# The normalisation of x in whole [128, 1024] tiles, its squares on ScalarE and its sums on VectorE

## The chip, the cores and the metric

The kernel runs on one core of a Trainium2 chip. Its time is the device time of one execution in microseconds; a figure for a kernel is the median of several executions. Engines are called as in the profile: PE is TensorE (matrix products), PEld its loading of weights, DVE is VectorE, ACT is ScalarE, POOL is GpSimd, SP is SyncE, which here issues the transfers.

## The reference, cut to what matters

One layer of an encoder works on `x` of 1024 tokens by 2048 features in float32. The input is normalised by its root mean square and multiplied by one large matrix, whose columns are split into the attention's parts and those of a state space model:

```
def rms_norm(x, g):
    y = x * rsqrt(mean(x * x, axis=-1) + EPS)
    return y * g

hn = rms_norm(h, norm_mix[i])
z = hn @ w_in[i]                      # 2048 x 4608
q, k, v, gate_a, u, gate_s = split(z)
```

Attention, the state space model, two more projections and a final norm follow; the change doesn't touch them.

## The kernel before, in words

The features lie on the partitions: `x` is 16 tiles of 128 features by 1024 tokens (step k = 0 to 15), and a column of the projection is 128 outputs. The kernel multiplies in two parts to keep float32 accuracy: a matrix X is split into H (X rounded to the type in which PE multiplies) and L (what is left of it), and a product is the sum of H·H, H·L and L·H. So a step k of a column is six products of 128 x 512, three for each half of the tokens (`mm_k`, lines 513 to 522): the weight's `wH` with `hH` (line 519) and `hL` (line 520), its `wL` with `hH` (line 522).

The scale by the gain `g` is folded into the split of `x`: `split` (lines 303 to 311) has ScalarE make `hH` = g·x (line 310) and VectorE make `hL` = g·x - `hH` (line 311). Weights go through the same helper without a gain: `wH` by ScalarE (line 307), `wL` by VectorE (line 308). The division by the root mean square comes later, on the columns' results. For it the squares of `x` are summed over the 16 tiles into `xsq` (128 x 1024) by `x_sq`; a product with ones then adds over the partitions (`x_rstd`, `colsum`).

The stage in question is the first loop of `run`. Two columns, `zf0` and `zf1`, are worked on at the same time, so a step is twelve products. Weights come in tiles of four steps each, two tiles (one for each column) for a block of four steps. In step k the program issues, in this order, the two columns' products, the load of tile k + 4 (`x_dma`), the split of tile k + 2 (`x_split`) and the square of tile k + 1 (`x_sq`); at k = 0, 4, 8, 12 `w_next` first loads and splits weights. Every engine takes its instructions in the order of the program, and waits where an operand or a buffer is not ready.

Three rings of buffers couple the engines. `xraw` has ten half tiles of 128 x 512, so a load of x waits until the tile five steps before has been split and squared. `wraw` has three tiles, so a weight load waits for the `wL` of an earlier tile; SyncE issues loads of x and of weights from one queue, and a waiting weight load holds up the loads of x behind it. `wH` and `wL` have four tiles each, so the casts for the next block wait until PE has finished the block before the current one's.

Before the change everything about x is done in half tiles: two loads, two `hH`, two `hL`. The first half of the tokens is squared and added by GpSimd (lines 493 and 495), the second half is squared by ScalarE (line 491) and added by VectorE (line 495). In step 0 ScalarE writes the squares of both halves straight into `xsq` (line 487).

Behind the stage come the third column (`zt`), with the parameters of the state space model as background work, the other columns, attention and the later projections.

Of the kernel before, what the change touches and what calls it, by code (L numbers as in the profile page):

```python
# [9 lines left out]
F32 = mybir.dt.float32  # L10
F32R = mybir.dt.float32r
I32 = mybir.dt.int32
ALU = mybir.AluOpType
AF = mybir.ActivationFunctionType
AX = mybir.AxisListType

SEQ = 1024
# [221 lines left out]
class Kernel:  # L239
# [223 lines left out]
    def x_dma(self, k):  # L463
        if k >= KD:
            return
        for h in range(2):
            xt = self.xp.tile([128, 512], F32, name="xraw", tag="xraw", bufs=10)
            self.nc.sync.dma_start(xt, self.i["xT"][k][:, self.half(h)])
            self.xraw.append(xt)

    def x_split(self, k):
        H = self.b4(f"hH{k}", dt=F32R)
        L = self.b4(f"hL{k}", dt=F32R)
        self.hH.append(H)
        self.hL.append(L)
        for h in range(2):
            s = self.half(h)
            self.split(H[:, s], L[:, s], self.xraw[2 * k + h], self.g_mix[:, k : k + 1])

    def x_sq(self, k):  # L480
        nc = self.nc
        for h in range(2):
            s = self.half(h)
            xt = self.xraw[2 * k + h]
            self.xraw[2 * k + h] = None
            if k == 0:
                nc.scalar.activation(self.xsq[:, s], xt, AF.Square)
                continue
            sq = self.xp.tile([128, 512], F32, name="xq", tag="xq", bufs=4)
            if h:  # L490
                nc.scalar.activation(sq, xt, AF.Square)
            else:
                nc.gpsimd.tensor_tensor(sq, xt, xt, ALU.mult)
            eng = nc.vector if h else nc.gpsimd
            eng.tensor_tensor(self.xsq[:, s], self.xsq[:, s], sq, ALU.add)

    def x_rstd(self):
        self.rstd = self.xsq
# [907 lines left out]
```

## Time and profile before

| | |
|---|---|
| median of 3 runs | 2195.66 us (2195.22 to 2196.39) |
| the profiled execution | 2196.16 us |
| its span | 2194.4 us |
| PE busy in it | 2129.4 us |
| DVE, ACT, POOL busy | 1384.1, 780.0, 656.0 us |

The span runs from the first to the last instruction that the profiler saw; the execution's time is 1.8 us longer. The products of PE overlap, so the distance between two starts says more than the duration of one. A row of the timeline merges neighbouring instructions of a kind (x2); the bracket at its end is the idle time of the engine before it and what ended it.

### The profile page before, as it was taken

How to read it: one execution, taken by the hardware profiler on the slowest of the kernel's cores; microseconds unless marked ns; L12 is line 12 of the kernel's file. 1: busy time of each engine (PE TensorE's matmuls, PEld its weight loads, DVE VectorE, ACT ScalarE, POOL GpSimd, SP SyncE). 2: the span in 40 equal slices, each digit the busy share in tenths (PEclk: the TensorE clock that was granted, in tenths of full speed). 3: DMA queues.
4: the chain of work that ended last, by engine and by line, in shares of the span. 5: the costliest groups of instructions: out<-in, count | busy, mean ns of one | idle time of the engine just before them, and what ended most of it. 6: DMA issues, size and time to landing. Idle time of an engine off the chain costs nothing.

```text
span 2194.4 us, 29198 instructions
## 1 busy us (share of the span) xinstructions
PE 2129.4 (97%) x10428; PEld 1777.3 (81%) x10428; DVE 1384.1 (63%) x2292; ACT 780.0 (36%) x1438; POOL 656.0 (30%) x630
## 2 busy tenths in 40 slices
PE   7999999999999999999999999999999999999996
PEld 5788878888887888887889888888887788888885
DVE  8745678787878787847999744444444644444344
ACT  5211222222222222237777633333334333333332
POOL 6152455555655554601222100111122000111120
PEclk8999999999999999999999999999999999999998
DMA  5224223323323333342121244444343644453333
GB/s 193 85 99 124 65 76 90 94 87 85 105 81 97 87 93 86 97 150 75 39 77 39 92 137 137 146 151 124 124 139 119 213 142 144 144 153 114 126 113 125
DMA packets 173313, 245.08 MB, mean 112 GB/s; under 512 B 27376, under 2 KB 77680, under 8 KB 172912
## 3 DMA queue, kind: packets, MB, share of 16 engines
q1 hardware_dynamic: 173168, 243.22, 35.6%
q8 instruction: 82, 1.34, 0.2%
q14 instruction: 63, 0.52, 0.1%
HBM read 189.35 MB, written 48.56 MB: 108 GB/s over the span
## 4 chain that ended last, share of the span: by engine, by line
PE 49%; DVE 3%; ACT 1%; DMA 1%; issue 1%; POOL 0%; DVEq 0%; SPq 0%; ACTq 0%
PE ph L1046 5%; PE ph L1047 5%; PE ph L1045 5%; PE pg L1047 5%; PE pg L1046 5%; PE pg L1045 5%; PE ptr L955 2%; PE pv L969 1%; PE pv L968 1%; PE pv L970 1%; PE S L925 1%; PE S L928 1%; PE S L924 1%; PE gg L1047 1%; PE gv L1047 1%; PE gv L1046 1%
## 5 line engine op out<-in xcount | busy, mean ns | idle before, releaser
L308 DVE TENSOR_TENSOR wL<-wraw,wH 128x512 fp32r<-128x512 f32 (+1 forms) x496 | 408.5, 844 | 451.1 <-ACT wH L307 449.5
L307 ACT CAST wH<-wraw 128x512 fp32r<-128x512 f32 (+1 forms) x496 | 294.0, 604 | 461.1 <-PE ph L1046 124.1
L1045 PE MATMUL pg<-hg,wH 128*128 128x512 f32 x512 | 200.8, 392 | 1.6 <-ACT wH L307 1.6
L1047 PE MATMUL pg<-hg,wL 128*128 128x512 f32 x512 | 199.9, 390 | 0.7 <-DVE wL L308 0.7
L1046 PE MATMUL pg<-hg,wH 128*128 128x512 f32 x512 | 199.7, 390 | 0.0
L1113 POOL TENSOR_TENSOR xsq<-xsq,tz 128x512 f32<-128x512 f32 x30 | 39.0, 1301 | 517.8 <-ACT tz L1112 517.8
L837 ACT COPY ks<-kp 16x224 f32<-16x224 f32 x32 | 10.8, 336 | 340.3 <-DVE ks L836 189.2
L1045 PEld LDWEIGHTS pg<-hg,wH 128*128 128x128 f32 x512 | 96.3, 188 | 22.4 <-ACT wH L307 2.0
L1047 PEld LDWEIGHTS pg<-hg,wL 128*128 128x128 f32 x512 | 96.4, 188 | 21.1 <-DVE wL L308 1.2
L1046 PEld LDWEIGHTS pg<-hg,wH 128*128 128x128 f32 x512 | 96.4, 188 | 20.5 <-issue 0.5
L519 PE MATMUL zga<-hH,wH 128*128 128x512 f32 x256 | 104.0, 406 | 0.0
L519 PE MATMUL zq<-hH,wH 128*128 128x512 f32 x256 | 103.5, 404 | 0.0
L519 PE MATMUL zgs<-hH,wH 128*128 128x512 f32 x256 | 102.6, 401 | 0.0
L520 PE MATMUL zq<-hL,wH 128*128 128x512 f32 x256 | 100.7, 394 | 0.0
L520 PE MATMUL zgs<-hL,wH 128*128 128x512 f32 x256 | 100.4, 392 | 0.0
L520 PE MATMUL zga<-hL,wH 128*128 128x512 f32 x256 | 100.2, 391 | 0.0
L1045 PE MATMUL ph<-ma,wH 128*128 128x512 f32 x256 | 99.6, 389 | 0.0
L1046 PE MATMUL ph<-ma,wH 128*128 128x512 f32 x256 | 99.6, 389 | 0.0
L1047 PE MATMUL ph<-ma,wL 128*128 128x512 f32 x256 | 99.6, 389 | 0.0
L1045 PE MATMUL ph<-ms,wH 128*128 128x512 f32 x256 | 99.6, 389 | 0.0
L1046 PE MATMUL ph<-ms,wH 128*128 128x512 f32 x256 | 99.6, 389 | 0.0
L1047 PE MATMUL ph<-ms,wL 128*128 128x512 f32 x256 | 99.6, 389 | 0.0
(420 smaller groups left out, 5432.6 us busy)
## 6 DMA issues: line engine op xcount, KB each, us to landing
wraw<-in_w_in_dram SPq DMA_DIRECT2D x144, 256.0 KB
wraw<-in_w_out_dram SPq DMA_DIRECT2D x128, 256.0 KB
wraw<-in_w_gate_dram SPq DMA_DIRECT2D x128, 256.0 KB
wraw<-in_w_glu_dram SPq DMA_DIRECT2D x64, 256.0 KB
xraw<-in_xT_dram SPq DMA_DIRECT2D x32, 256.0 KB
out_dram<-h SPq DMA_DIRECT2D x32, 256.0 KB
t<-zz SPq DMA_DIRECT2D x40, 128.0 KB
d_u<-tz SPq DMA_DIRECT2D x16, 256.0 KB
```

The lines of the kernel that those rows point to most:

```text
L307: nc.scalar.copy(H, src)
L308: nc.vector.tensor_tensor(L, src, H.bitcast(F32), ALU.subtract)
L519: nc.tensor.matmul(ps[h], H[:, kk, :], rH[:, s], start=(k == 0), stop=False)
L520: nc.tensor.matmul(ps[h], H[:, kk, :], rL[:, s], start=False, stop=False)
L924: nc.tensor.matmul(S[:, s], qH[:, qs], kH[:, s], start=True, stop=False)
L925: nc.tensor.matmul(S[:, s], qH[:, qs], kL[:, s], start=False, stop=False)
L928: nc.tensor.matmul(S[:, s], qL[:, qs], kH[:, s], start=False, stop=True)
L955: nc.tensor.transpose(pc[:, b], P[:, 512 * hf + 128 * b : 512 * hf + 128 * b + 128], self.ident)
L1045: nc.tensor.matmul(ps, H[:, k % 4], x[:, 0], start=(k == 0), stop=False)
L1046: nc.tensor.matmul(ps, H[:, k % 4], x[:, 1], start=False, stop=False)
L1047: nc.tensor.matmul(ps, L[:, k % 4], x[:, 0], start=False, stop=(k == nk - 1))
L1113: nc.gpsimd.tensor_tensor(acc, acc, s2, ALU.add)
```

## The change

A tile of x is one buffer of 128 x 1024 (five of them), filled by one load, split by one instruction on each engine and squared by one on ScalarE; VectorE adds the whole square into `xsq`. Only tile 0 is still loaded and split in two halves. GpSimd has no part in it any more.

```diff
     def x_dma(self, k):
         if k >= KD:
             return
-        for h in range(2):
-            xt = self.xp.tile([128, 512], F32, name="xraw", tag="xraw", bufs=10)
-            self.nc.sync.dma_start(xt, self.i["xT"][k][:, self.half(h)])
-            self.xraw.append(xt)
+        xt = self.xp.tile([128, SEQ], F32, name="xraw", tag="xraw", bufs=5)
+        for s in [self.half(0), self.half(1)] if k == 0 else [slice(0, SEQ)]:
+            self.nc.sync.dma_start(xt[:, s], self.i["xT"][k][:, s])
+        self.xraw.append(xt)
 
     def x_split(self, k):
...
-        for h in range(2):
-            s = self.half(h)
-            self.split(H[:, s], L[:, s], self.xraw[2 * k + h], self.g_mix[:, k : k + 1])
+        for s in [self.half(0), self.half(1)] if k == 0 else [slice(0, SEQ)]:
+            self.split(H[:, s], L[:, s], self.xraw[k][:, s], self.g_mix[:, k : k + 1])
 
     def x_sq(self, k):
         nc = self.nc
-        for h in range(2):
-            s = self.half(h)
-            xt = self.xraw[2 * k + h]
-            self.xraw[2 * k + h] = None
-            if k == 0:
-                nc.scalar.activation(self.xsq[:, s], xt, AF.Square)
-                continue
-            sq = self.xp.tile([128, 512], F32, name="xq", tag="xq", bufs=4)
-            if h:
-                nc.scalar.activation(sq, xt, AF.Square)
-            else:
-                nc.gpsimd.tensor_tensor(sq, xt, xt, ALU.mult)
-            eng = nc.vector if h else nc.gpsimd
-            eng.tensor_tensor(self.xsq[:, s], self.xsq[:, s], sq, ALU.add)
+        xt = self.xraw[k]
+        self.xraw[k] = None
+        if k == 0:
+            nc.scalar.activation(self.xsq, xt, AF.Square)
+            return
+        sq = self.xp.tile([128, SEQ], F32, name="xq", tag="xq", bufs=2)
+        nc.scalar.activation(sq, xt, AF.Square)
+        nc.vector.tensor_tensor(self.xsq, self.xsq, sq, ALU.add)
```

The program before, VectorE's queue from the split of block 1's weights on (then tiles 2 to 4 of x; the number behind a name tells the tiles apart):

```order
L308 TENSOR_TENSOR wL<-wraw,wH 128x512 x2
L311 SCALAR_TENSOR_TENSOR hL_260<-xraw,vec,hH_259 128x512 x2
L495 TENSOR_TENSOR xsq<-xsq,xq 128x512
L311 SCALAR_TENSOR_TENSOR hL_288<-xraw,vec,hH_287 128x512 x2
L495 TENSOR_TENSOR xsq<-xsq,xq 128x512
L311 SCALAR_TENSOR_TENSOR hL_316<-xraw,vec,hH_315 128x512 x2
L495 TENSOR_TENSOR xsq<-xsq,xq 128x512
```

The same place of VectorE's queue now:

```order
L308 TENSOR_TENSOR wL<-wraw,wH 128x512 x2
L311 SCALAR_TENSOR_TENSOR hL_248<-xraw,vec,hH_247 128x1024
L488 TENSOR_TENSOR xsq<-xsq,xq 128x1024
L311 SCALAR_TENSOR_TENSOR hL_269<-xraw,vec,hH_268 128x1024
L488 TENSOR_TENSOR xsq<-xsq,xq 128x1024
L311 SCALAR_TENSOR_TENSOR hL_290<-xraw,vec,hH_289 128x1024
L488 TENSOR_TENSOR xsq<-xsq,xq 128x1024
```

The sequence is the same; two instructions of 512 columns for `hL` have become one of 1024, and each add has twice the columns.

ScalarE's queue before, from the split of tile 2 to the weights behind tile 5:

```order
L310 ACTIVATE hH_259<-xraw,vec 128x512 x2
L491 ACTIVATE xq<-xraw 128x512
L310 ACTIVATE hH_287<-xraw,vec 128x512 x2
L491 ACTIVATE xq<-xraw 128x512
L310 ACTIVATE hH_315<-xraw,vec 128x512 x2
L491 ACTIVATE xq<-xraw 128x512
L310 ACTIVATE hH_343<-xraw,vec 128x512 x2
L491 ACTIVATE xq<-xraw 128x512
L307 CAST wH<-wraw 128x512 x2
```

The same place of ScalarE's queue now:

```order
L310 ACTIVATE hH_247<-xraw,vec 128x1024
L487 ACTIVATE xq<-xraw 128x1024
L310 ACTIVATE hH_268<-xraw,vec 128x1024
L487 ACTIVATE xq<-xraw 128x1024
L310 ACTIVATE hH_289<-xraw,vec 128x1024
L487 ACTIVATE xq<-xraw 128x1024
L310 ACTIVATE hH_310<-xraw,vec 128x1024
L487 ACTIVATE xq<-xraw 128x1024
L307 CAST wH<-wraw 128x512 x2
```

Again the sequence stays; each square covers the whole tile instead of its second half.

## Rows read from the trace of the kernel before

**Rows 1.** The page: span, and busy time of each engine with its share.

```profile
span 2194.4 us, 29198 instructions
PE 2129.4 (97%) x10428; PEld 1777.3 (81%) x10428; DVE 1384.1 (63%) x2292; ACT 780.0 (36%) x1438; POOL 656.0 (30%) x630
```

**Rows 2.** Stretches: length; PE, PEld, DVE, ACT, POOL busy (count); PEclk; DMA; GB/s.

```profile
6.08:74.64 68.56, 55.93 (x193) 41.79 (x194) 63.52 (x58) 35.88 (x59) 46.46 (x34) 0.88 0.45 156
47.20:63.62 16.42, 13.08 (x50) 9.84 (x49) 16.42 (x15) 8.82 (x15) 12.28 (x8) 0.90 0.48 160
74.64:200.00 125.36, 125.36 (x559) 103.37 (x558) 75.97 (x269) 14.30 (x25) 32.83 (x61) 1.00 0.34 108
...
20.00:22.00 2.00, 2.00 (x6) 1.57 (x5) 2.00 (x3) 2.00 (x4) 1.92 (x2) 0.50 1.05 390
```

**Rows 3.** Waits of PE, 0 to 75 us: total, times, longest.

```profile
PE zf L520 <- DVE hL L311: 12.6, 8, 2.9
```

**Rows 4.** Timeline of PE: start, length, instruction, [idle before and its end].

```profile
17.22 0.80 PE L520 MATMUL zf<-hL,wH 128*128 128x512 f32 x1 [2.06 <-DVE hL L311]
...
26.20 0.39 PE L519 MATMUL zf<-hH,wH 128*128 128x512 f32 x1
...
43.22 0.39 PE L519 MATMUL zf<-hH,wH 128*128 128x512 f32 x1
...
44.58 0.40 PE L519 MATMUL zf<-hH,wH 128*128 128x512 f32 x1
...
58.01 0.39 PE L519 MATMUL zf<-hH,wH 128*128 128x512 f32 x1
...
74.64 0.39 PE L519 MATMUL zt<-hH,wH 128*128 128x512 f32 x1
```

**Rows 5.** Timeline of VectorE.

```profile
26.98 2.19 DVE L311 SCALAR_TENSOR_TENSOR hL<-xraw,vec,hH 128x512 fp32r<-128x512 f32 x2
29.09 1.78 DVE L495 TENSOR_TENSOR xsq<-xsq,xq 128x512 f32<-128x512 f32 x1
30.79 2.13 DVE L308 TENSOR_TENSOR wL<-wraw,wH 128x512 fp32r<-128x512 f32 x2
...
35.17 0.68 DVE L495 TENSOR_TENSOR xsq<-xsq,xq 128x512 f32<-128x512 f32 x1
...
68.00 0.68 DVE L495 TENSOR_TENSOR xsq<-xsq,xq 128x512 f32<-128x512 f32 x1
68.60 1.41 DVE L311 SCALAR_TENSOR_TENSOR hL<-xraw,vec,hH 128x512 fp32r<-128x512 f32 x2
69.93 1.48 DVE L495 TENSOR_TENSOR xsq<-xsq,xq 128x512 f32<-128x512 f32 x2
```

**Rows 6.** Timeline of GpSimd.

```profile
35.93 1.48 POOL L493 TENSOR_TENSOR xq<-xraw 128x512 f32<-128x512 f32 x1 [1.89 <-DVE xsq L495]
...
71.52 0.09 POOL L671 MEMSET sgn<- 64x1 f32 x1 [4.65 <-DVE xsq L495]
```

**Rows 7.** Groups by form, whole span: count, busy us, mean ns, idle before.

```profile
L935 DVE TENSOR_REDUCE mx<-S 128x1 f32<-128x1024 f32 x64 | 78.1, 1221 | 9.3 <-PE S L928 9.2
L308 DVE TENSOR_TENSOR wL<-wraw,wH 128x256 fp32r<-128x256 f32 x32 | 13.2, 413 | 1.3 <-ACT wH L307 1.3
L308 DVE TENSOR_TENSOR ms<-tz,ms 128x512 fp32r<-128x512 f32 x16 | 11.1, 693 | 9.0 <-ACT ms L307 8.9
...
L307 ACT CAST wH<-wraw 128x512 fp32r<-128x512 f32 x464 | 284.1, 618 | 458.9 <-PE ph L1046 124.1 <-DMA wraw<-in_w_gate_dram 91.0 <-PE zu L520 52.1
L307 ACT CAST wH<-wraw 128x256 fp32r<-128x256 f32 x32 | 12.9, 402 | 2.2 <-DMA wraw<-in_w_proj_dram 2.2
```

**Rows 8.** Timeline of ScalarE.

```profile
12.60 1.26 ACT L307 CAST wH<-wraw 128x512 fp32r<-128x512 f32 x2 [1.51 <-DMA wraw<-in_w_in_dram]
...
35.47 1.43 ACT L310 ACTIVATE hH<-xraw,vec 128x512 fp32r<-128x512 f32 x2 [5.40 <-DMA xraw<-in_xT_dram]
```

**Rows 9.** Timeline of SyncE's queue: start, time over all of the issues.

```profile
31.88 3.76 SPq L468 DMA_DIRECT2D xraw<-in_xT_dram  x8
```

## The prediction

> **What bounds the kernel now.** I read the page first: a span of 2194.4 us, TensorE (PE) busy for 2129.4 us of it [rows 1]. So PE sets the time, and a change in the first 75 us counts only where PE stands idle or runs slowly there. The busy time by stretch comes next [rows 2]. The stage that the change touches, the first two columns of the input projection (`zf`), runs from 6.08 to 74.64 us, 68.56 us in which PE was busy for 55.9, at a mean granted clock of 0.88; in the 125 us behind it PE is busy all the time, at 1.00. The list of waits says for whom PE stood idle inside the stage: 12.6 us for the VectorE line that makes `hL` [rows 3].
>
> The timeline of PE gives what the stage could take [rows 4]. Six products start at 43.22 and the next six at 44.58, so a product takes 1.36 / 6 = 0.2267 us at 2.4 GHz. A block of four steps k (two columns of six products each) is 48 products or 10.88 us, the stage 192 or 43.5 us: 25 us are lost. Block 0 ends at 26.20, block 2 at 58.01, block 3 at 74.64: 31.8 us for blocks 1 and 2 together, 16.6 for block 3.
>
> VectorE is what the blocks keep pace with: from 47.20 to 63.62, one block of its own, it is busy for 16.42 of 16.42 us [rows 2]. Its timeline has the same instruction at two speeds [rows 5]. While GpSimd works, two halves of `hL` take 2.1 us and half an add into `xsq` 1.70 (29.09 to 30.79); GpSimd has been idle for 4.65 us when its instruction of 71.52 starts [rows 6], and in that gap the half add takes 0.60 (68.00 to 68.60) and the two halves of `hL` 1.33 (68.60 to 69.93). One step costs VectorE 3.81 us beside GpSimd (26.98 to 30.79) and 1.93 without it.
>
> **The change, part by part.**
>
> *GpSimd's squares and adds go* (15 of each). GpSimd is on no path of PE here, so its time itself is worth nothing; what goes is the slowing of VectorE, about 1.9 us a step.
>
> *VectorE gets the other half of each add, in one instruction, and `hL` in one instead of two.* No row shows these at 1024 columns. The slope comes from the subtraction of a split, 0.413 us at 256 columns and 0.693 at 512 [rows 7]: 0.56 us for 512 columns more. A whole add is then 0.60 + 0.56 = 1.16 us, a whole `hL` 0.665 + 0.56 = 1.225. A block is 4 x 2.385 + 2 weight subtractions x 0.69 = 10.9 us. Bounds: two halves each at the undisturbed price, 4 x 2.53 + 1.38 = 11.5 us; below, a reduction over 1024 columns at 1.22 us [rows 7], less the 0.08 by which 0.68 exceeds 0.60, for both: 4 x 2.28 + 1.38 = 10.5. I take 10.9, because the slope is that of the same kind of instruction.
>
> The Trainium skill speaks against this part: "Perfetto Trace Analysis", section "Optimizing Scalar/DVE Operations", says that a saturated VectorE is a reason to move work away from it, even to GpSimd; the change moves half of the adds onto it. The same section adds that moving work between these two might not help, as they share a read port. By the first rule alone the result would be that of the slower rival below; the trace's two speeds bear out the second, so the sum keeps 10.9.
>
> *ScalarE squares whole tiles.* Its slope is (0.618 - 0.402) / 256 columns [rows 7], 0.43 us for 512 more: a whole square about 1.05 us, a whole `hH` 0.71 (half of the 1.43 for two [rows 8]) + 0.43 = 1.14, a block 2 x 0.62 + 4 x 2.2 = 10.0 us, at most (two halves each) 1.24 + 4 x 2.57 = 11.5. Spacing is shorter than duration, so the first is high. It lies beside PE's 10.88. ScalarE now squares 32 halves instead of 17, and waits for nothing in that but its own queue.
>
> *One load per tile.* The loads of the next four tiles stand in SyncE's queue behind a weight load that waits for a weight subtraction (at 31.88 [rows 9]). The first half of the first tile landed by 35.47, and its second half by the time ScalarE reached it 0.7 us later [rows 8]: 4.3 us for a whole tile. After the change, counted from PE's end of a block (the casts of the next weights wait for that): weight cast 0.62, subtraction 0.69, issue of the weight load 0.47 (3.76 / 8 [rows 9]), tile 4.3, `hH` 1.14, `hL` 1.31, together 8.5 us; PE wants that tile one block later, at 10.9. So 2.4 us of cover. With that cover gone each late microsecond counts once per block, in the three blocks that such bursts feed (tiles 4 to 7, 8 to 11, 12 to 15).
>
> *Block 0.* Before, the first product with `hL` of step 2 starts at 17.22 after 2.06 us of idleness, and the 23 products left need 9.0 us to 26.20 [rows 4], where 23 x 0.2267 = 5.2 would do: the granted clock was 0.50 behind that idleness, six products from 20 to 22 us [rows 2]. After, the weight casts end at about 13.8 (12.60 + 1.26 [rows 8]), `hH` at 14.9, `hL` at 16.2, since VectorE has no backlog; PE still waits for it, by two shorter stretches, and may run at 1.2 GHz again. End of block 0: 16.2 + 5.2 = 21.4 at 2.4 GHz, 25.2 with the same slow stretch as before; if the weights land sooner behind fewer transfers (ScalarE waited 1.51 us for them [rows 8]), 19.9. I take 23.0, the middle of the two nearest cases.
>
> *Blocks 1 to 3.* The longer of PE's 10.88 and VectorE's 10.9, plus 0.2 because two engines of the same pace meet at several places: 11.1 each, bounds 10.9 and 11.7.
>
> *Behind the stage.* The last add of `xsq` was done at 71.4 [rows 5] and its column sums were due two steps behind 74.64. After, VectorE ends some 3 us before PE again, and the queue orders behind it are the same, so everything later moves forward as a whole.
>
> **Sum.** 23.0 + 3 x 11.1 = 56.3 us instead of 74.64: 18.3 us less. The profiled execution took 2196.16 us, 1.8 over its span, and the median of the runs is 0.5 below it: 2196.2 - 18.3 - 0.5 = 2177.4, given as 2177.
>
> **Rivals.**
>
> *Slower: VectorE is slow whoever else works.* If the high price of its instructions came from ScalarE or the transfers, the moved half of an add would cost its busy price: 1.70 us in each of 15 steps [rows 5], 25.5 us, and 2221 us. It decides from the point where whole `hL` instructions take over 2 us with GpSimd empty. For it: in the gap at 68 to 70 us ScalarE and the transfers were quiet as well. Against it: the half add at 35.17 also took 0.68, as at 68.00 [rows 5], between two pieces of GpSimd's work (idle for 1.89 us before 35.93 [rows 6]), while ScalarE was at `hH` and a load had just landed (35.47 [rows 8]).
>
> *Loads late.* If a whole tile lands 2 us beyond the 2.4 of cover, blocks last about 13: 23.0 + 39 = 62, a gain of 12.6 and 2183 us. For it: a tile can be used only when all of it is there, and a block now asks for its 2.6 MB (four tiles of 512 KB, two weight loads) in 11 us instead of 16.6. Against it: the landing time above.
>
> *VectorE stays the bound, narrowly.* Blocks of 11.7, two more us in all, 2179. For it: its sum and PE's differ by nothing. Against: the bounds of 10.5 and 11.5 lie around PE's pace.
>
> *Given back.* A later chain that doesn't start from this stage would take the gain; 2196. Against it: PE has no idle time at all in the 125 us behind the stage [rows 2], and all queues move with it.
>
> **How the numbers follow.** Forecast 0.70, its own range 2174 to 2180 (block 0 from 19.9 to 25.2); loads late 0.13; VectorE narrowly 0.12; slower 0.03; given back 0.02. The range of 2173.5 to 2183.5 holds the first three but for the worst of the loads. About 0.2%, 4.4 us, is what a measurement of this kernel can tell from no change: faster 0.70 + 0.13 + 0.12 = 0.95, same 0.02, slower 0.03.
>
> **What would show it.** `hL` and `xsq` of 1024 columns at 1.2 to 1.3 us each, no VectorE instruction of the stage near 1.7 per 512 columns; blocks of PE of 10.9 to 11.3 us; the third column starting at 54 to 59 us instead of 74.64; the granted clock at 1.00 from block 1 on; the stretch behind it as long as before. Wrong, if ScalarE waits for `xraw` and PE for `hH`, if the `hL` rows stay above 2 us, or if PE waits longer behind the stage by as much as it gained.

## The result and the profile after

The changed kernel took 2175.23 us (median of 4 runs, 2171.39 to 2178.28) against 2196.02 for the kernel before, a ratio of 0.9905 (95% interval 0.9887 to 0.9922): 20.8 us faster, where 2177 was forecast. On two further occasions its ratio was 0.9906 (0.9891 to 0.9921) and 0.9897 (0.9880 to 0.9913).

The page of the changed kernel, answering to [rows 1]:

```profile
span 2172.4 us, 29077 instructions
PE 2119.5 (98%) x10428; PEld 1771.1 (82%) x10428; DVE 1362.9 (63%) x2277; ACT 782.8 (36%) x1422; POOL 611.9 (28%) x600
```

PE does the same 10428 products in 9.9 us less busy time, and the span is 22.0 us shorter. VectorE has 15 instructions less and is busy for 21 us less, although it adds 15 x 512 columns more.

The stretches of the changed kernel, answering to [rows 2]: the stage, its blocks 1 and 2, and the 125 us behind it (columns as there).

```profile
6.11:55.65 49.54, 47.48 (x193) 36.47 (x193) 42.60 (x41) 38.65 (x43) 0.44 (x4) 1.00 0.60 213
32.74:44.03 11.29, 11.23 (x50) 8.93 (x48) 10.27 (x10) 8.76 (x11) 0.00 (x0) 1.00 0.67 229
55.65:181.01 125.36, 125.36 (x559) 103.37 (x558) 76.28 (x270) 14.31 (x25) 32.92 (x62) 1.00 0.35 110
21.79:32.74 10.95, 10.95 (x49) 8.93 (x48) 10.29 (x11) 8.78 (x11) 0.00 (x0) 1.00 0.62 224
```

The stage lasts 49.54 us instead of 68.56, 19.0 less; the granted clock is 1.00 instead of 0.88 in it. The 125.36 us behind it hold the same 559 products in both kernels, with PE busy throughout. The waits of PE in the first 60 us, answering to [rows 3], show the other half of the gain:

```profile
PE zf L512 <- ACT hH L310: 6.3, 2, 6.1
PE zf L513 <- DVE hL L311: 1.6, 2, 0.8
```

6.1 us of the first row are the start of the kernel, so inside the stage PE waited 1.8 us instead of 12.6, 10.8 less. A clock of 0.88 over 68.56 us had cost about 0.12 x 68.56 = 8.2 us. Together 19.0.

The timeline of VectorE over a block, answering to [rows 5]:

```profile
36.13 1.28 DVE L308 TENSOR_TENSOR wL<-wraw,wH 128x512 fp32r<-128x512 f32 x2
37.33 1.27 DVE L311 SCALAR_TENSOR_TENSOR hL<-xraw,vec,hH 128x1024 fp32r<-128x1024 f32 x1
38.52 1.22 DVE L488 TENSOR_TENSOR xsq<-xsq,xq 128x1024 f32<-128x1024 f32 x1
39.66 1.28 DVE L311 SCALAR_TENSOR_TENSOR hL<-xraw,vec,hH 128x1024 fp32r<-128x1024 f32 x1
40.86 1.22 DVE L488 TENSOR_TENSOR xsq<-xsq,xq 128x1024 f32<-128x1024 f32 x1
43.09 1.29 DVE L311 SCALAR_TENSOR_TENSOR hL<-xraw,vec,hH 128x1024 fp32r<-128x1024 f32 x1 [1.02 <-ACT hH L310]
```

A whole `hL` and a whole add come 1.20 and 1.13 us apart, a step is 2.33 us where it was 3.81. There is one speed now. But VectorE waits 1.02 us for an `hH`, and that `hH` for its tile, as the timelines of ScalarE and of SyncE's queue show:

```profile
30.27 1.15 ACT L310 ACTIVATE hH<-xraw,vec 128x1024 fp32r<-128x1024 f32 x1 [2.17 <-DMA xraw<-in_xT_dram]
...
41.91 1.15 ACT L310 ACTIVATE hH<-xraw,vec 128x1024 fp32r<-128x1024 f32 x1 [2.53 <-DMA xraw<-in_xT_dram]
```

```profile
18.37 7.51 SPq L393 DMA_DIRECT2D wraw<-in_w_in_dram  x2
25.93 2.51 SPq L468 DMA_DIRECT2D xraw<-in_xT_dram  x4
...
37.22 2.52 SPq L468 DMA_DIRECT2D xraw<-in_xT_dram  x4
```

Four loads of x leave at 25.93, behind the weight loads, and the first tile is there at 30.27; the next four leave at 37.22, and their first tile is there at 41.91.

### The profile page after: what moved, and what is told of

Its sections match the earlier page's. It is cut to its first block, busy times and chain, and to the rows that moved or that the text cites. A ratio compares the mean times of both kernels' runs of the same rounds, so it can differ in the third digit from the quotient of the medians.

```text
span 2172.4 us, 29077 instructions
## 1 busy us (share of the span) xinstructions
PE 2119.5 (98%) x10428; PEld 1771.1 (82%) x10428; DVE 1362.9 (63%) x2277; ACT 782.8 (36%) x1422; POOL 611.9 (28%) x600
## 4 chain that ended last, share of the span: by engine, by line
PE 50%; DVE 3%; ACT 1%; issue 1%; DMA 1%; POOL 0%; DVEq 0%; SPq 0%; ACTq 0%
PE ph L1040 5%; PE ph L1039 5%; PE ph L1038 5%; PE pg L1040 5%; PE pg L1038 5%; PE pg L1039 5%; PE ptr L948 2%; PE pv L962 1%; PE pv L961 1%; PE pv L963 1%; PE S L918 1%; PE S L921 1%; PE S L917 1%; PE gg L1040 1%; PE gv L1038 1%; PE gv L1039 1%
```

## The experiments

All start from one of the two kernels. The last column but one is the start of the third column, which is the end of the stage; the last is the span less that.

| kernel | median, us | ratio to before (95%) | third column | behind it |
|---|---|---|---|---|
| before, three profiles | 2196.0 | 1 | 74.64, 75.38, 74.26 | 2119.8, 2121.6, 2120.7 |
| changed, three profiles | 2175.2, 2175.5, 2175.1 | 0.9905, 0.9906, 0.9897 | 55.65, 55.52, 55.08 | 2116.8, 2116.8, 2116.1 |
| halves, no GpSimd | 2176.4 | 0.9917 (0.9903 to 0.9930) | 55.41 | 2116.4 |
| whole tiles, GpSimd kept | 2196.0 | 0.9999 (0.9988 to 1.0010) | 72.02 | 2120.2 |
| first three tiles in halves | 2176.2 | 0.9910 (0.9897 to 0.9924) | 55.50 | 2117.9 |
| the same, x ahead of weights | 2176.2 | 0.9902 (0.9886 to 0.9919) | 54.29 | 2117.5 |

Each ratio is to the kernel before on the same occasion; its medians were 2196.0, 2196.8 and 2199.0 us.

**GpSimd's part alone.** Half tiles everywhere as before, but every square on ScalarE and every sum on VectorE:

```diff
-            if h:
-                nc.scalar.activation(sq, xt, AF.Square)
-            else:
-                nc.gpsimd.tensor_tensor(sq, xt, xt, ALU.mult)
-            eng = nc.vector if h else nc.gpsimd
-            eng.tensor_tensor(self.xsq[:, s], self.xsq[:, s], sq, ALU.add)
+            nc.scalar.activation(sq, xt, AF.Square)
+            nc.vector.tensor_tensor(self.xsq[:, s], self.xsq[:, s], sq, ALU.add)
```

> Loads, splits, squares and sums in half tiles as before, but all squares on ScalarE and all sums on VectorE. Theory (GpSimd slows VectorE): every hL half at 0.66 us spacing and every half add at 0.60; VectorE's block 4 x 2.53 + 1.24 = 11.4 us, a little over PE's 10.88, so the third column starts at 57 to 58 us and the time is 1 to 3 us over the changed kernel's. Rival (whole tiles are what helps): VectorE stays at 3.8 us or more a step, the third column starts at 74 us or later.

The timeline of VectorE in that kernel, over one block, and the end of the stage on PE:

```profile
36.48 1.28 DVE L308 TENSOR_TENSOR wL<-wraw,wH 128x512 fp32r<-128x512 f32 x2
37.69 1.41 DVE L311 SCALAR_TENSOR_TENSOR hL<-xraw,vec,hH 128x512 fp32r<-128x512 f32 x2
39.01 1.28 DVE L491 TENSOR_TENSOR xsq<-xsq,xq 128x512 f32<-128x512 f32 x2
...
47.80 1.29 DVE L308 TENSOR_TENSOR wL<-wraw,wH 128x512 fp32r<-128x512 f32 x2
```

```profile
55.41 0.39 PE L515 MATMUL zt<-hH,wH 128*128 128x512 f32 x1
```

Two halves cost VectorE 1.32 and 1.20 us, a block 11.32 (36.48 to 47.80), as expected. Even so the third column starts at 55.41, not at 57 to 58: the halves let PE begin sooner, and block 0 ended at 20.76 instead of 21.79. This part alone brings the whole gain as far as the times can tell (0.9917 beside 0.9905); merging the halves is not needed for it.

**The merging alone.** Whole tiles, with GpSimd squaring and adding the first half:

```diff
-        sq = self.xp.tile([128, SEQ], F32, name="xq", tag="xq", bufs=2)
-        nc.scalar.activation(sq, xt, AF.Square)
-        nc.vector.tensor_tensor(self.xsq, self.xsq, sq, ALU.add)
+        for h in range(2):
+            s = self.half(h)
+            sq = self.xp.tile([128, 512], F32, name="xq", tag="xq", bufs=4)
+            if h:
+                nc.scalar.activation(sq, xt[:, s], AF.Square)
+            else:
+                nc.gpsimd.tensor_tensor(sq, xt[:, s], xt[:, s], ALU.mult)
+            eng = nc.vector if h else nc.gpsimd
+            eng.tensor_tensor(self.xsq[:, s], self.xsq[:, s], sq, ALU.add)
```

> Whole tiles for loads and splits as in the changed kernel, but GpSimd squares and adds the first half of each tile as before. Theory (GpSimd slows VectorE): a step of VectorE stays near 3.6 to 3.8 us, blocks of 15 to 16.5 us, the third column at 71 to 75 us, time as before the change within 4 us. Rival (whole tiles help): blocks under 12 us, the third column by 60 us.

VectorE in that kernel:

```profile
33.31 2.28 DVE L311 SCALAR_TENSOR_TENSOR hL<-xraw,vec,hH 128x1024 fp32r<-128x1024 f32 x1
35.51 0.68 DVE L494 TENSOR_TENSOR xsq<-xsq,xq 128x512 f32<-128x512 f32 x1
36.12 1.27 DVE L311 SCALAR_TENSOR_TENSOR hL<-xraw,vec,hH 128x1024 fp32r<-128x1024 f32 x1
37.31 1.52 DVE L494 TENSOR_TENSOR xsq<-xsq,xq 128x512 f32<-128x512 f32 x1
38.76 2.30 DVE L311 SCALAR_TENSOR_TENSOR hL<-xraw,vec,hH 128x1024 fp32r<-128x1024 f32 x1
40.98 1.52 DVE L494 TENSOR_TENSOR xsq<-xsq,xq 128x512 f32<-128x512 f32 x1
```

GpSimd in it, behind its work that ended at 34.51:

```profile
36.76 1.53 POOL L492 TENSOR_TENSOR xq<-xraw 128x512 f32<-128x512 f32 x1 [2.25 <-DMA xraw<-in_xT_dram]
```

The same `hL` takes 2.28 us beside GpSimd and 1.27 when it starts at 36.12 with GpSimd idle, in one kernel and three microseconds apart. Beside GpSimd a half add and an `hL` together take 3.67 us (37.31 to 38.76 and, at 2.22, to 40.98), and the time is that of the kernel before.

**Is it the work on GpSimd, or that the engines wait for each other's data?** Three variants of the changed kernel give the idle GpSimd work that nobody reads, on a private tile, in each of the 16 steps. They were run once each (2198.1 us with products, 2184.1 with memsets, 2187.2 with copies), and GpSimd's work outlasts the stage and delays what follows, so their traces are read and not their times.

```diff
+        da = self.xp.tile([128, 384], F32, name="da", tag="da", bufs=1)
+        self.nc.gpsimd.memset(da, 1.0)
...
+            for _ in range(3):     # or 8 x memset(da, 1.0), or 4 x tensor_copy(da, da)
+                self.nc.gpsimd.tensor_tensor(da, da, da, ALU.mult)
```

> The changed kernel with 48 products of 128x384 on GpSimd in the stage (a private tile times itself, nobody reads it, nobody waits). They add work to no other engine. Theory (a GpSimd instruction that reads operands slows VectorE): from about 8 to 55 us hL of 1024 columns takes 2 us or more instead of 1.28 and xsq 1.8 or more instead of 1.22; a step of VectorE goes from 2.34 to about 4 us and the third column starts at 70 us or later. Rival (before, VectorE and GpSimd were slow because they waited for each other's data): hL and xsq stay at 1.28 and 1.22, the third column at 55.5.

> The same with 128 memsets of 128x384 on GpSimd, which write the private tile and read nothing. If reading is what collides, hL and xsq stay at 1.28 and 1.22 us and the third column starts at 55.5 us; if any work on GpSimd collides, VectorE is slowed as with the products.

> The same with 64 copies of 128x384 on GpSimd (one operand read instead of two). If any reading collides, hL and xsq are slowed while the copies run, by less per copy than per product if the time held is that of the instruction; if only two operands collide, they stay at 1.28 and 1.22 us and the third column at 55.5.

VectorE's groups by form from 14 to 48 us (count, busy us, mean ns), with the products:

```profile
L488 DVE TENSOR_TENSOR xsq<-xsq,xq 128x1024 f32<-128x1024 f32 x8 | 14.8, 1845 | 0.0
L311 DVE SCALAR_TENSOR_TENSOR hL<-xraw,vec,hH 128x1024 fp32r<-128x1024 f32 x8 | 14.8, 1845 | 0.0
```

With the copies:

```profile
L311 DVE SCALAR_TENSOR_TENSOR hL<-xraw,vec,hH 128x1024 fp32r<-128x1024 f32 x11 | 16.3, 1486 | 0.2 <-ACT hH L310 0.2
L488 DVE TENSOR_TENSOR xsq<-xsq,xq 128x1024 f32<-128x1024 f32 x10 | 15.2, 1519 | 0.0
```

With the memsets:

```profile
L311 DVE SCALAR_TENSOR_TENSOR hL<-xraw,vec,hH 128x1024 fp32r<-128x1024 f32 x12 | 15.4, 1283 | 2.4 <-ACT hH L310 2.4
L488 DVE TENSOR_TENSOR xsq<-xsq,xq 128x1024 f32<-128x1024 f32 x12 | 14.7, 1221 | 0.0
```

The same 34 us as a stretch (columns as in [rows 2]), first with the products, then with the copies, then with the memsets:

```profile
14.00:48.00 34.00, 25.48 (x102) 18.15 (x101) 34.00 (x21) 22.64 (x24) 32.35 (x22) 1.00 0.44 155
```

```profile
14.00:48.00 34.00, 29.55 (x122) 21.71 (x121) 33.76 (x26) 23.69 (x26) 32.40 (x27) 1.00 0.63 219
```

```profile
14.00:48.00 34.00, 32.86 (x141) 25.78 (x140) 31.59 (x31) 28.30 (x32) 29.91 (x72) 1.00 0.64 232
```

Nobody waits for GpSimd's work, and beside the products VectorE is busy without a pause (34.00 of 34.00 us), so it waits for nobody; its instructions still go from 1.28 and 1.22 us to 1.85, and the third column starts at 75.00, as late as in the kernel before. Copies cost less (1.5 us, 61.69), memsets nothing (1.28 and 1.22, 55.88), though GpSimd is busy for 32.4, 32.4 and 29.9 us in the three. So the slowing comes from what GpSimd executes, not from waiting nor from how long it is busy, and that rival falls. The price follows the operands that GpSimd reads (two, one, none); the three kinds differ in what they compute as well, which no run here tells apart. The expected 2 us were a little high: a step is 3.53 us, not 4.

**What stretches blocks 1 to 3?** They took 10.95, 11.29 and 11.62 us, and only PE's 10.88 is given by its own work. First the start was made earlier, by halves in the first three tiles:

```diff
-        for s in [self.half(0), self.half(1)] if k == 0 else [slice(0, SEQ)]:
+        for s in [self.half(0), self.half(1)] if k < 3 else [slice(0, SEQ)]:
```

> The changed kernel with tiles 0, 1 and 2 loaded and split in halves instead of tile 0 alone. PE waited 0.8 us for hL of step 1 and 1.0 us at step 2 in the changed kernel; a first half is ready about 0.55 us sooner on each of two engines, so the third column starts 0.7 to 1.6 us earlier, at 54.0 to 55.0 us, and the time follows if no half-speed period is added. Rival: the added instructions (two on ScalarE, two on VectorE, 0.1 us each) push the later tiles back and the start is where it was.

It missed: block 0 ended 0.8 us earlier, at 20.95, but the blocks behind it took 11.27, 11.45 and 11.83, and the third column started at 55.50. The time gained at the start was given back bit by bit: step 6 began 0.78 us sooner than in the changed kernel, step 12 0.36, the third column 0.15. VectorE's waits for the late tiles grew meanwhile from 0.66 and 1.02 us to 0.83 and 1.22. Then the load of the next tile was moved ahead of the weight loads of steps 4 and 8 as well:

```diff
+            early = k > 0 and k % 4 == 0
+            if early:
+                self.x_dma(k + 4)
             if k % 4 == 0:
                 w = [self.w_next(), self.w_next()]
             for n in range(2):
                 self.mm_k(first[n], w[n], k % 4, k)
-            self.x_dma(k + 4)
+            if not early:
+                self.x_dma(k + 4)
```

> The kernel with tiles 0 to 2 in halves, and in steps 4 and 8 the load of the next tile of x issued ahead of the two weight loads instead of behind them. In the changed kernel VectorE stood idle 0.7 and 1.0 us in blocks 1 and 2 until a tile had landed and its hH was made; if that wait is what stretched blocks 1 to 3 to 11.3 and 11.6 us, it goes, blocks are 10.9 to 11.1 us each and the third column starts at 53.5 to 54.3 us, 1.3 to 2 us before the changed kernel's 55.6. Rival (VectorE's own work is what stretches them): blocks stay at 11.3 to 11.8 and the third column at 55.4. In the time of the whole this is at the limit of what can be told.

Blocks 2 and 3 of that kernel, as stretches:

```profile
32.53:43.41 10.88, 10.88 (x50) 9.01 (x48) 10.88 (x12) 9.36 (x12) 0.00 (x0) 1.00 0.72 249
43.41:54.29 10.88, 10.88 (x50) 9.01 (x48) 9.45 (x10) 7.06 (x8) 0.53 (x4) 1.00 0.09 29
```

Both last 10.88 us with PE busy throughout. VectorE doesn't wait in block 2, and its weight subtractions of three blocks start at 24.62, 35.15 and 45.68, so its own work for a block is 10.53 us. Block 1 still took 11.35: its `hL` of tile 6 is done only at 27.11, and PE's product with it starts 0.3 us late, at 27.16. VectorE had lost 0.35 us to a late tile at 19.96; that this is why was not tested. So it was the waiting load that stretched blocks 2 and 3. The stage ends 1.2 us before that of the kernel with halves alone, from which this one differs in nothing else, and 0.8 us before that of the changed kernel beside it on the same chip (54.29 against 55.08). The changed kernel's own three profiles lie 0.6 us apart there, and its third missed the expected 55.5 to 55.7, so the two blocks of 10.88 us are the better evidence. The times of the whole can't tell: 2176.2 and 2175.1.

> The changed kernel unaltered beside it on the same chip, for a comparison of the two: third column at 55.5 to 55.7 us, time within 2 us of its other medians, 2175.2 and 2175.5, if chips don't differ.

**The 3 us behind the stage.** The changed kernel gained 19.0 us in the stage and 22.0 in the span.

> The changed kernel unaltered, for a second profile and more times. Inside the first 60 us nothing should differ (third column starts at 55.6 to 55.7 us). The first profile gained 19.0 us in the stage and 3.0 us behind it, where the granted clock kept at 1.00 at 280 us and stood at 0.50 for one period before. If that part belongs to the change, the second profile has it too; if it is chance, the half-speed periods behind the stage lie elsewhere or differ in number, and the time moves with them by about 1.7 us each.

> The kernel before, unaltered, for a second profile of it. In the first one 2119.8 us lay between the start of the third column and the end; in the three profiles of the changed kernel 2116.1 to 2116.8. If those 3 us are a matter of where half-speed periods happen to fall, this profile's part behind the stage lies anywhere between 2116 and 2121; if they belong to the change, it is 2119.5 us or more again.

> A third profile of the kernel before, for the same question and with the same expectation.

The table's last column has 2119.8 to 2121.6 for the kernel before and for the one that keeps GpSimd, and 2116.1 to 2117.9 for those without it in the stage, with no overlap. That speaks against chance alone. But the difference arises at several places, and not at the same ones in each profile. One is shown by the stretches around 300 us before and about the same work 20 us earlier after, the kernel before first:

```profile
295.00:306.00 11.00, 7.61 (x37) 6.17 (x36) 7.88 (x6) 0.92 (x2) 8.90 (x6) 0.84 0.28 93
```

```profile
275.00:286.00 11.00, 8.94 (x52) 7.32 (x51) 7.80 (x7) 1.55 (x3) 9.82 (x8) 1.00 0.30 96
```

Before, PE got through 37 products there with the clock at 0.84 behind a wait, after, 52 at 1.00. But the place doesn't decide it: in the changed kernel's third profile it ran at 0.84 too, and yet no profile has less behind the stage (2116.1).

```profile
275.00:286.00 11.00, 8.47 (x43) 6.90 (x42) 7.66 (x7) 1.48 (x3) 9.67 (x8) 0.84 0.30 97
```

What makes the 3 us stays open.

## Why the prediction was right, step by step

- **What goes with GpSimd.** Predicted: about 1.9 us a step of VectorE's slowing. Measured: a step went from 3.81 to 2.33 us although it has half an add more. The two speeds in one trace were read rightly, and the products that nobody reads show the cause.
- **VectorE's instructions.** Predicted 1.225 and 1.16 us apart, measured 1.20 and 1.13; weight subtractions 0.60 and not 0.69, which was a duration where a spacing was wanted. A block is 10.53 us, near the lower bound of 10.5, not 10.9.
- **ScalarE.** Predicted 1.14 and 1.05 us, measured 1.14 and 1.05 in the mean. Its pace is off the path. (The upper bound of 11.5 is a slip: two halves of each come to 1.43 + 1.24 = 2.67 us and not 2.57, so it is 11.9. Nothing hangs on it.) ScalarE did wait for `xraw`, 2.17 and 2.53 us, which was named as half of a sign of being wrong; the other half, PE waiting for `hH`, came to 0.20 us.
- **One load per tile.** Predicted 4.3 us from issue to use, measured 4.34 (25.93 to 30.27) and 4.69 (37.22 to 41.91). The cover of 2.4 us was not there. It counted the weight cast and the subtraction as if they began as soon as PE was done with a block. PE's block 0 ended at 21.79, but both engines were still at work on x:

```profile
22.98 1.12 ACT L307 CAST wH<-wraw 128x512 fp32r<-128x512 f32 x2
```

```profile
24.85 1.28 DVE L308 TENSOR_TENSOR wL<-wraw,wH 128x512 fp32r<-128x512 f32 x2
...
31.45 1.28 DVE L311 SCALAR_TENSOR_TENSOR hL<-xraw,vec,hH 128x1024 fp32r<-128x1024 f32 x1 [0.66 <-ACT hH L310]
```

  So the loads of x left 4.14 us behind the block's end and not 1.78, and `hL` was done at 32.73, 10.94 us behind it and not 8.5, just as PE began the block that needs it (32.74). A block later it was done at 44.38, and PE's product with it started about 0.2 us late, at 44.43. VectorE, which reaches such a tile before PE does, loses up to 1.02 us there, in a queue with only 10.88 - 10.53 = 0.35 us to spare. So a small part of the rival "loads late" came true, though the tiles landed about on time: it is the 0.4 and 0.7 us that blocks 2 and 3 took over 10.9.
- **Block 0.** Predicted to end at 23.0, a value between a case without a slow stretch (21.4) and one with it (25.2), whose middle is 23.3; it ended at 21.79, so the first case came. `hL` was done at 16.34, where 16.2 was reckoned. PE's two waits of that place were shorter than the 2.06 us of before, as forecast, and the granted clock stayed at 1.00:

```profile
12.09 0.50 PE L513 MATMUL zf<-hL,wH 128*128 128x512 f32 x1 [0.83 <-DVE hL L311]
...
15.08 0.50 PE L512 MATMUL zf<-hH,wH 128*128 128x512 f32 x1 [0.20 <-ACT hH L310]
16.40 0.50 PE L513 MATMUL zf<-hL,wH 128*128 128x512 f32 x1 [0.82 <-DVE hL L311]
...
21.79 0.39 PE L512 MATMUL zf<-hH,wH 128*128 128x512 f32 x1
...
55.65 0.39 PE L512 MATMUL zt<-hH,wH 128*128 128x512 f32 x1
```

- **Blocks 1 to 3.** Predicted 3 x 11.1 = 33.3, measured 33.86, for the reason told under the loads and not because PE and VectorE are equally fast. Block 3, with 11.62, lies outside the 10.9 to 11.3 that were given as a sign.
- **Sum.** 56.3 predicted, 55.65 measured: -1.2 in block 0, +0.6 in the others. That the two partly cancel is luck.
- **Behind the stage.** VectorE's last add of the stage was done at 55.04, 0.6 us before PE and not 3, as it now runs almost at PE's pace; the column sums came at 58.37 all the same. The prediction gave nothing to what follows, where 3.0 us more were gained: this is the step it missed, and 2175.2 instead of 2177 is mostly that.
- **The rivals.** "VectorE is slow whoever else works" fell with the first row of VectorE. "VectorE stays the bound, narrowly" is false by its own work, 10.53 against 10.88, though with the waits for late tiles its queue did stretch block 3 to 11.62. "Given back" is false: behind the stage PE does the same 559 products in the same 125.36 us, and the span gained more than the stage.

## What to carry to other kernels

An instruction that has two speeds in one trace names its rival: look at what else runs in its slow rows and what is idle in its fast ones, and price the change with the fast ones. Moving work onto the busiest engine can make that engine faster, if the work leaves a neighbour that slows it. After such a gain the next limit is close: count it with spacings and not with durations, and look at who uses a late operand first, which need not be the engine that sets the time.

## What the runs showed of the hardware that was not expected

- How much GpSimd slows a VectorE instruction depends on what GpSimd executes. Per VectorE instruction of 1024 columns: 0.6 us beside products of two operands at 384 columns, 0.2 to 0.3 beside copies, none beside memsets.
- Beside products, `hL` and the add come at the same 1.77 us from each other, though alone they need 1.20 and 1.13: the pair of engines falls into one rhythm. GpSimd is slowed as well; its products took 0.83 us at the least and 1.69 in the median (minimum, median and maximum in ns):

```profile
L1255 POOL TENSOR_TENSOR da<-da x48: 827/1687/1692, 2.3 to 74.6; 128x384 f32<-128x384 f32 x48
```

  The extra 0.6 us of VectorE is less than a whole product on GpSimd, of which the first four, almost all before VectorE's first instruction at 5.32, took 3.54 us in a row, 0.89 each.
- Three waits of PE of 0.83, 0.20 and 0.82 us within 5 us left the granted clock at 1.00, where one of 2.06 had been followed by 0.50.
- A granted clock of 1.00 doesn't say that the first products ran at full speed: they come 0.43 us apart in both kernels (7.46, 7.89 and 8.31 before, 7.49, 7.92 and 8.34 after), as at 0.50 later (20.35 and 20.77 before), against 0.23 at 1.00.
